# Attention's values in one stationary tile: two passes instead of three, and the sums of the probabilities added on GpSimd

## The chip, the cores and the metric

The kernel runs on one core of a Trainium2 chip. The time is the device time of one execution in microseconds, the median of several runs. The core's engines work side by side and are named as the profile names them: PE (TensorE, matrix products; PEld is its loading of the stationary operand), DVE (VectorE), ACT (ScalarE), POOL (GpSimd) and SP (SyncE, which issues most DMAs). Each engine works off its own queue in order and waits on semaphores for the others.

## The reference

A trunk of two layers on 1024 rows of 1024 numbers, in float32. Layer 0 mixes with a gated MLP, layer 1 with attention; each is followed by a channel mixer (an up-projection, a short convolution, a gate, a down-projection). The change lies in the attention:

```python
def one_chunk(args):
    c, qb = args
    start = c * CHUNK
    kb = lax.dynamic_slice_in_dim(kp, start, BAND, axis=1)
    vb = lax.dynamic_slice_in_dim(vp, start, BAND, axis=1)
    sc = jnp.einsum('bqhd,bkhd->bhqk', qb, kb).astype(jnp.float32) + bias
    ...
    p = jax.nn.softmax(sc, axis=-1).astype(vb.dtype)
    return jnp.einsum('bhqk,bkhd->bqhd', p, vb)
```

There are 16 heads of 64 numbers. Each chunk of 64 rows sees itself and the 8 chunks before it, so a block of 128 keys is seen by at most five blocks of 128 queries.

## The kernel before

**Precision.** PE multiplies in a format with fewer bits than float32 (`F32R`). So each operand is split into a high part (a cast, on ACT) and a low part (the difference, on DVE or POOL), and a product is made of three passes: high by high, low by high, high by low. The helper `split` does this (lines 137 to 140: `hi` by ACT, `lo` by DVE), which is why many rows of the profile bear L139 and L140.

**The attention's tiles.** Two heads make a pair `p` of 128 columns; `c` is 0 or 1 within the pair, and a head number is 2p + c. `rows[c]` gives the head's own 64 partitions and the other 64. The values of a pair come from a projection (`operand`, L1088 and around), are transposed on PE (`transpose_v`) and split into `vh` and `vl`. The stationary tile of a head and key block has 128 columns: 64 hold the head's values, the other 64 hold ones (in `VH`) or zeros (in `VL`). So the product of `VH` with the probabilities gives in 64 rows the weighted values and in the other 64 the sum of the probabilities, which the softmax divides by. The values of the second head are put into their tile by two DMAs (`stage_v`).

**A head's steps.** `Head.score(kb)` makes, for key block kb (0 to 7), the scores `st` of up to five query blocks (up to 640 columns) on PE, adds the bias near the diagonal on DVE, takes the exponential on ACT (tile `p`, two instructions), casts it to `ph` on ACT (L1269) and subtracts to `pl` on POOL (L1270). `Head.value(kb)` multiplies: for each half `t` of the 1024 query columns that the block touches, three passes into the PSUM tile `po` (L1286 `vh` by `ph`, L1288 `vl` by `ph`, L1290 `vh` by `pl`). The first half is complete with block 3, the second with block 7. Then `Pair.done` copies the sum of the probabilities to `den` (ACT, L1311) and the values to `o` (DVE, L1315); later, with delays counted in a modelled clock (`put_off`), `o` is multiplied by the reciprocal of `den`.

**The order of the work.** PE's order is written out by hand: `tick` counts a modelled time of PE, and what was put off is issued when its time has come. The other engines' queues are ordered by the framework's scheduler, which knows nothing of the chip's real times. The main loop goes over s, 16 heads by 8 blocks. A step issues the scores of block i, half of the step's projection matmuls (`fill`: those of the next pair's q, k and v), the row maxima of the next head (`mx`, DVE), then `value` of the block two steps back (`LAG = 2`), then the other half. A step has 12 projection matmuls in the first head of a pair and 6 in the second; about 5 in pair 0 and in the last pair, and 3 in the first half of head 13. The projections' weights come by DMA and are scaled by a gain on POOL (L159), one of 1024 columns per weight. The small PSUM tiles (`psS`: `st`, `mx`, transposes) rotate through four banks, `po` through two.

Of the kernel before, what the change touches and what calls it, by code (L numbers as in the profile page):

```python
# [10 lines left out]
F32 = mybir.dt.float32  # L11
F32R = mybir.dt.float32r
AF = mybir.ActivationFunctionType
ALU = mybir.AluOpType
# [4 lines left out]
P = 128  # L19
T = 1024  # L20
D = 1024
H = 512
KD = D // P
NB = T // P
# [5 lines left out]
LAG = 2  # L30
# [11 lines left out]
def f32(ap):  # L42
    return ap.bitcast(F32)
# [3 lines left out]
def trunk(ctx: ExitStack, tc: tile.TileContext, x, a_win, a_wv, a_wst, a_bs, a_wout, w_kv, w_q, w_o,  # L47
          f_win, f_wdown, bias, cst, consts, fgain, out):
    nc = tc.nc
    V, S, G = nc.vector, nc.scalar, nc.gpsimd  # L50
# [78 lines left out]
    ones_r = cp.tile([P, P], F32R, name="ones_r")  # L129
# [7 lines left out]
    def split(hi, lo, src, eng=V):  # L137

        behind[S] = S.copy(hi, src)  # L139
        return eng.tensor_tensor(lo, src, f32(hi), op=ALU.subtract)  # L140
# [444 lines left out]
    for t in range(2):  # L585
        for n in range(4):
            ps = psA("vps")
# [49 lines left out]
    for i, g in enumerate((0, 4, 1, 5, 2, 6, 3, 7)):  # L637
# [3 lines left out]
        for t in range(2):  # L641
            spatial(g, t)
            ps = psA("ups")
# [404 lines left out]
    rows = [(slice(0, 64), slice(64, P)), (slice(64, P), slice(0, 64))]  # L1048
# [19 lines left out]
    parts = {}  # L1068

    def operand(p, what, w, t):  # L1070

        hs = halves[t]
        if t == 0:
            if what == "v":
                parts[p, what] = [b1.tile([P, NB, 64], F32R, tag=f"v{n}", name=f"v{n}") for n in ("hi", "lo")]
            else:
                parts[p, what] = [bt.tile([P, T], F32R, tag=f"t{n}", name=f"t{n}") for n in ("hi", "lo")]
        hi, lo = parts[p, what]
        if p == 0:
            ps = ps2[what, t]  # L1080
        else:
            ps = psP("qkv")
            yield from products(ps, w, ys[t], range(KD), LAST)
        if what == "q":
            S.mul(hi[:, hs], ps, 0.125)
            V.scalar_tensor_tensor(lo[:, hs], ps, 0.125, f32(hi[:, hs]), op0=ALU.mult, op1=ALU.subtract)
        elif what == "k":
            S.copy(hi[:, hs], ps)  # L1088
            V.tensor_tensor(lo[:, hs], ps, f32(hi[:, hs]), op=ALU.subtract)
        else:  # L1090
            vT = b2.tile([P, H], F32, tag="vT", name="vT")
            S.copy(vT, ps)
            put_off(1.2, lambda: transpose_v(vT, t, hi, lo))

    def stage(hd, cs):

# [45 lines left out]
    LAST = KD - 1  # L1142
# [13 lines left out]
    with tc.tile_pool(name="b1", bufs=1, reuse_waits="tile") as b1, \  # L1156
# [2 lines left out]

        for place, n in ((QE, "qe"), (QS, "qs"), (KM, "km"), (KS, "ks")):  # L1160
            place.append(b1.tile([P, T], F32R, name=f"{n}1"))
        VH, VL = ([b1.tile([P, NB, P], F32R, name=f"{n}{c}") for c in range(2)] for n in ("vh", "vl"))
        constant_rows(1, lambda: b2.tile([P, H], F32, tag="o", name="e"))
        for c in range(2):
            oth = rows[c][1]
            G.memset(f32(VH[c][:, :, oth]), 1.0)
            G.memset(f32(VL[c][:, :, oth]), 0.0)

        def heads():

# [5 lines left out]
                    yield from operand(p, what, w, t)  # L1176
                w = nw

        def transpose_v(vT, t, hi, lo):
            pt = psS("vtr")  # L1180
            for i in range(4):
                nc.tensor.transpose(pt[:, i * P:(i + 1) * P], vT[:, i * P:(i + 1) * P], ident)
            ns = slice(t * 4, t * 4 + 4)
            ptv = pt.rearrange("p (n c) -> p n c", c=P)
            for c, vh, vl in ((0, VH[0][:, ns, 0:64], VL[0][:, ns, 0:64]), (1, hi[:, ns, :], lo[:, ns, :])):
                src = ptv[:, :, rows[c][0]]
                S.copy(vh, src)
                V.tensor_tensor(vl, src, f32(vh), op=ALU.subtract)

        def stage_v(p):  # L1190
            for dst, src in zip((VH[1], VL[1]), parts[p, "v"]):
                nc.sync.dma_start(f32(dst[:, :, 64:P]), f32(src))

        class Max:

# [38 lines left out]
        class Head:  # L1234


            def __init__(self, hd, bt, done):
                self.hd, self.c, self.bt, self.done = hd, hd % 2, bt, done
                self.po = [None, None]
                self.p = {}  # L1240

            def score(self, kb):
# [19 lines left out]
                marks[0] = V.tensor_tensor(pf[:, :n2], near[:, :n2], bt[:, :n2], op=ALU.add)  # L1262
                S.activation(pf[:, :n2], pf[:, :n2], AF.Exp)
# [5 lines left out]
                marks[1] = S.copy(ph[:, :n], pf[:, :n])  # L1269
                marks[2] = G.tensor_tensor(pl[:, :n], pf[:, :n], f32(ph[:, :n]), op=ALU.subtract)  # L1270
                self.p[kb] = (ph, pl)

            def value(self, kb):

                c, (ph, pl) = self.c, self.p.pop(kb)
                q0 = kb * P
                lo_end = q0 + min(5, NB - kb) * P
                for t, (a, b) in enumerate(((q0, min(lo_end, H)), (max(q0, H), lo_end))):
# [7 lines left out]
                    nc.tensor.matmul(d, VH[c][:, kb, :], ph[:, r], start=kb == 0, stop=False, skip_group_check=True)  # L1286
                    tick(d.shape[1])
                    nc.tensor.matmul(d, VL[c][:, kb, :], ph[:, r], start=False, stop=False, skip_group_check=True)  # L1288
                    tick(d.shape[1])
                    nc.tensor.matmul(d, VH[c][:, kb, :], pl[:, r], start=False, stop=last, skip_group_check=True)  # L1290
                    tick(d.shape[1])
                    if last:
                        self.done(c, t, self.po[t])

        class Pair:

# [2 lines left out]
                self.p = p  # L1299
                self.o, self.den = [None, None], [None, None]  # L1300

            def done(self, c, t, po):
# [4 lines left out]
                p = self.p  # L1307
                if p < LAST:

                    row = slice(oth.start, oth.start + 1)  # L1310
                    S.copy(self.den[t][row], po[row])  # L1311
                    nc.sync.dma_start(dens[p][t][0][c:c + 1], self.den[t][row])
                else:
                    S.copy(self.den[t][own], po[oth])
# [80 lines left out]
        mid, end = {2: (1,), 3: (3,), 4: (5,), 5: (7,)}, {1: (0,), 2: (2,), 3: (4,), 4: (6,)}  # L1395
        for s in range(NH * NB):
            hd, i = divmod(s, NB)
            p, c = divmod(hd, 2)
# [5 lines left out]
            n = (6 if c else 12) + (1 - 2 * c if i == 0 else 0)  # L1404
            if p == LAST - 1 and c:
                n = 3 if i < 4 else 6
            if p == 0:
                n = (144 - early) * (s + 1) // 16 - (144 - early) * s // 16
            if p == LAST:
                n = 5  # L1410
# [27 lines left out]
            if i == (LAG if p < LAST else 5) and c == 0:  # L1438
                stage_v(p)
            for _ in range(n // 2):  # L1440
                next(fill, None)
            if hd + 1 < NH:
# [189 lines left out]
```

## Time and profile before

| | us |
|---|---|
| median of 3 runs (2134.68 to 2136.11) | 2135.33 |
| span of the profiled execution | 2131.1 |
| median over that span | 4.2 |
| POOL L1270 `pl`, 128 instructions, busy | 161.1 |
| first and last pass L1290 start at | 987.0, 1409.8 |

The span runs from the first to the last instruction of the one execution that the profiler recorded; a run's time has some microseconds around it, and the profiled execution's own time is known only as this span. In the rows of the profile, a timeline's row gives the start, the duration, the engine, the line, the operation, what it writes and reads with the shapes, and, in brackets, how long the engine stood idle before it and who ended that. A row that begins with two times gives, for that stretch, each engine's busy time with its number of instructions, then the granted clock of PE as a share of full speed, the DMA share and GB/s.

### The profile page before, as it was taken

How to read it: one execution, taken by the hardware profiler on the slowest of the kernel's cores; microseconds unless marked ns; L12 is line 12 of the kernel's file. 1: busy time of each engine (PE TensorE's matmuls, PEld its weight loads, DVE VectorE, ACT ScalarE, POOL GpSimd, SP SyncE). 2: the span in 40 equal slices, each digit the busy share in tenths (PEclk: the TensorE clock that was granted, in tenths of full speed). 3: DMA queues.
4: the chain of work that ended last, by engine and by line, in shares of the span. 5: the costliest groups of instructions: out<-in, count | busy, mean ns of one | idle time of the engine just before them, and what ended most of it. 6: DMA issues, size and time to landing. Idle time of an engine off the chain costs nothing.

```text
span 2131.1 us, 28842 instructions
## 1 busy us (share of the span) xinstructions
PE 2116.7 (99%) x9944; PEld 1773.0 (83%) x9944; DVE 1545.7 (73%) x2311; ACT 1065.4 (50%) x1878; POOL 752.9 (35%) x530
## 2 busy tenths in 40 slices
PE   9999999999999999999999999999999999999998
PEld 8888877888888888888888888888888888888887
DVE  4188789888888856675665655665988888885576
ACT  6333555545455544555555555643545544454443
POOL 1075745242333412054545444421322323341020
PEclk9999999999999999999999999999999999999999
DMA  7257722354445976735554555663243545478653
GB/s 253 79 203 256 243 99 99 130 193 138 163 165 194 296 269 215 239 105 139 139 127 129 129 130 133 178 218 114 73 154 134 186 137 175 164 278 300 213 190 126
DMA packets 181450, 367.86 MB, mean 173 GB/s; under 512 B 42908, under 2 KB 43292, under 8 KB 181304
## 3 DMA queue, kind: packets, MB, share of 16 engines
q1 hardware_dynamic: 177128, 358.47, 51.8%
q10 hardware_dynamic: 4176, 7.55, 1.0%
q8 instruction: 78, 1.28, 0.3%
q14 instruction: 68, 0.56, 0.1%
HBM read 233.12 MB, written 103.40 MB: 158 GB/s over the span
## 4 chain that ended last, share of the span: by engine, by line
PE 93%; DVE 4%; POOL 1%; ACT 1%; issue 1%; DMA 0%; DVEq 0%; SPq 0%; POOLq 0%; ACTq 0%
PE up L995 10%; PE gate L995 10%; PE up L375 7%; PE up L377 7%; PE up L380 7%; PE gate L375 5%; PE gate L377 5%; PE gate L380 5%; PE vps L510 4%; PE qkv L184 4%; PE qkv L181 4%; PE qkv L188 4%; PE ups L181 1%; PE po L1290 1%; PE st L1256 1%; PE ups L184 1%
## 5 line engine op out<-in xcount | busy, mean ns | idle before, releaser
L140 DVE TENSOR_TENSOR wlo<-raw,whi 128x512 fp32r<-128x512 f32 (+1 forms) x395 | 343.7, 876 | 179.8 <-ACT whi L139 179.6
L139 ACT CAST whi<-raw 128x512 fp32r<-128x512 f32 (+1 forms) x395 | 245.0, 623 | 282.7 <-PE gate L995 198.5
L375 PE MATMUL up<-yh,whi 128*128 128x512 f32 x688 | 267.8, 389 | 0.0
L377 PE MATMUL up<-yh,wlo 128*128 128x512 f32 x688 | 267.8, 389 | 0.0
L1270 POOL TENSOR_TENSOR pl<-p,ph 128x640 fp32r<-128x640 f32 (+4 forms) x128 | 161.1, 1261 | 180.1 <-ACT ph L1269 134.4
L847 POOL TENSOR_TENSOR h<-a 128x512 f32<-128x512 f32 x44 | 80.6, 1832 | 398.7 <-DVE a L839 387.3
L375 PE MATMUL gate<-th,whi 128*128 128x512 f32 x496 | 193.9, 391 | 2.7 <-DVE gate L903 2.7
L377 PE MATMUL gate<-th,wlo 128*128 128x512 f32 x496 | 193.9, 391 | 0.0
L380 PE MATMUL up<-yl,whi 128*128 128x512 f32 x688 | 184.2, 389 | 0.0
L380 PEld LDWEIGHTS up<-yl,whi 128*128 128x128 f32 x688 | 129.2, 188 | 27.2 <-POOL yl L140 0.5
L375 PEld LDWEIGHTS up<-yh,whi 128*128 128x128 f32 x688 | 129.2, 188 | 27.1 <-ACT gate L886 0.3
L377 PEld LDWEIGHTS up<-yh,wlo 128*128 128x128 f32 x688 | 129.2, 188 | 26.8
L140 DVE TENSOR_TENSOR yl<-raw,yh 128x512 fp32r<-128x512 f32 x172 | 143.1, 834 | 8.4 <-ACT yh L139 8.2
L184 PE MATMUL qkv<-yh,wlo 128*128 128x512 f32 x336 | 134.3, 400 | 0.0
L380 PE MATMUL gate<-tl,whi 128*128 128x512 f32 x496 | 132.7, 389 | 0.0
L181 PE MATMUL qkv<-yh,whi 128*128 128x512 f32 x336 | 132.5, 394 | 0.0
L139 ACT CAST whi<-S 128x512 fp32r<-128x512 f32 x160 | 99.0, 619 | 65.0 <-PE up L380 59.0
L140 DVE TENSOR_TENSOR wlo<-S,whi 128x512 fp32r<-128x512 f32 x160 | 130.2, 814 | 0.0
L995 PE MATMUL up<-yl,whi 128*128 128x512 f32 (+1 forms) x312 | 120.6, 387 | 0.0
L995 PE MATMUL up<-yh,whi 128*128 128x512 f32 (+1 forms) x312 | 120.4, 386 | 0.0
L995 PE MATMUL gate<-yh,wlo 128*128 128x512 f32 (+1 forms) x312 | 120.4, 386 | 0.0
L995 PE MATMUL up<-yh,wlo 128*128 128x512 f32 (+1 forms) x312 | 120.3, 386 | 0.0
(306 smaller groups left out, 5274.6 us busy)
## 6 DMA issues: line engine op xcount, KB each, us to landing
raw<-in_f_win SPq DMA_DIRECT2D x88, 512.0 KB
gT<-h SPq DMA_DIRECT2D x88, 256.0 KB
h<-in_f_wdown SPq DMA_DIRECT2D x44, 512.0 KB
dS<-h SPq DMA_DIRECT2D x88, 256.0 KB
raw<-dS SPq DMA_DIRECT2D x40, 512.0 KB
raw<-gT SPq DMA_DIRECT2D x40, 512.0 KB
gB<-a SPq DMA_DIRECT2D x66, 256.0 KB
raw<-in_f_wdown SPq DMA_DIRECT2D x30, 512.0 KB
```

Of the source, the lines that this page charges most:

```text
L139: behind[S] = S.copy(hi, src)
L140: return eng.tensor_tensor(lo, src, f32(hi), op=ALU.subtract)
L181: nc.tensor.matmul(ps, wh[:, k, :], xs[k][0], start=k == 0, stop=False)
L184: nc.tensor.matmul(ps, wl[:, k, :], xs[k][0], start=False, stop=False)
L188: nc.tensor.matmul(ps, wh[:, k, :], xs[k][1], start=False, stop=k == last)
L375: nc.tensor.matmul(ps, wh[:, k, :], xs[k][0], start=first and k == 0, stop=False, skip_group_check=True)
L377: nc.tensor.matmul(ps, wl[:, k, :], xs[k][0], start=False, stop=False, skip_group_check=True)
L380: nc.tensor.matmul(ps, wh[:, k, :], xs[k][1], start=False, stop=k == 3, skip_group_check=True)
L510: nc.tensor.matmul(ps, a, b, start=k == i == 0, stop=k == KD - 1 and i == 2)
L847: G.tensor_tensor(B[n], x, B.get(y) if isinstance(y, str) else y, op=ALU.subtract)
L995: nc.tensor.matmul(ps[:, cs], w[:, ms], x[:, cs], start=q == i == 0 and p in (1, 6, 5, 4), stop=q == NP - 1 and i == 2, skip_group_check=True)
L1270: marks[2] = G.tensor_tensor(pl[:, :n], pf[:, :n], f32(ph[:, :n]), op=ALU.subtract)
```

## The change

The stationary tile of a head and key block now holds the high part of the values in the head's own 64 columns and the low part in the other 64. One pass with `ph` and one with `pl` then give high and low products in the two halves of `po`, and `Pair.done` adds the halves (ACT copies one half to `o`, DVE adds the other). The passes with `vl` are gone. The second head's tile is doubled (`V1`) instead of being filled by DMA, so `stage_v` is gone.

The sums of the probabilities are no longer a by-product. `score` adds each block's `p` on POOL into `sum[t]` (a copy for block 0, a memset for the second half, adds for the rest). After block 3 (first half) and block 7 (second half) the sum is split into `sumh` (ACT) and `suml` (DVE), and `total`, called at the end of `value` for block 3 and block 7, multiplies both with a tile of ones: two passes of 512 columns into a small PSUM bank, `den`.

```diff
-        VH, VL = ([b1.tile([P, NB, P], F32R, name=f"{n}{c}") for c in range(2)] for n in ("vh", "vl"))
+        V0, *V1 = (b1.tile([P, NB, P], F32R, name=f"v{n}") for n in ("0", "1a", "1b"))
...
-            for c, vh, vl in ((0, VH[0][:, ns, 0:64], VL[0][:, ns, 0:64]), (1, hi[:, ns, :], lo[:, ns, :])):
-                src = ptv[:, :, rows[c][0]]
+            for v, (own, oth) in zip(both, rows):
+                src, vh = ptv[:, :, own], v[:, ns, own]
                 S.copy(vh, src)
-                V.tensor_tensor(vl, src, f32(vh), op=ALU.subtract)
+                V.tensor_tensor(v[:, ns, oth], src, f32(vh), op=ALU.subtract)
...
                 self.p[kb] = (ph, pl)
+                for t, (a, b) in enumerate(self.ranges(kb)):
+                    if a >= b:
+                        continue
+                    d, e = self.sum[t][:, a - t * H:b - t * H], pf[:, a - q0:b - q0]
+                    if kb == t == 0:
+                        G.tensor_copy(d, e)
+                        G.memset(self.sum[1], 0.0)
+                    else:
+                        G.tensor_tensor(d, d, e, op=ALU.add)
+                    if kb == (NB - 1 if t else 3):
+                        self.parts = [b2.tile([P, H], F32R, tag=n, name=n, bufs=1) for n in ("sumh", "suml")]
+                        split(*self.parts, self.sum[t])
...
+            def total(self, t):
+                ps = psS("den")
+                for i in range(2):
+                    nc.tensor.matmul(ps, ones_r, self.parts[i], start=i == 0, stop=i == 1)
+                    tick()
+                return ps
...
-                    nc.tensor.matmul(d, VH[c][:, kb, :], ph[:, r], start=kb == 0, stop=False, skip_group_check=True)
+                    nc.tensor.matmul(d, self.v[:, kb, :], ph[:, r], start=kb == 0, stop=False, skip_group_check=True)
                     tick(d.shape[1])
-                    nc.tensor.matmul(d, VL[c][:, kb, :], ph[:, r], start=False, stop=False, skip_group_check=True)
-                    tick(d.shape[1])
-                    nc.tensor.matmul(d, VH[c][:, kb, :], pl[:, r], start=False, stop=last, skip_group_check=True)
+                    nc.tensor.matmul(d, self.v[:, kb, :], pl[:, r], start=False, stop=last, skip_group_check=True)
                     tick(d.shape[1])
                     if last:
-                        self.done(c, t, self.po[t])
+                        self.done(c, t, self.po[t], self.total(t))
...
-                    S.copy(self.den[t][row], po[row])
+                    S.copy(self.den[t][row], total[row])
...
-                V.tensor_copy(self.o[t][own], po[own])
+                S.copy(self.o[t][own], po[oth])
+                V.tensor_tensor(self.o[t][own], po[own], self.o[t][own], op=ALU.add)
```

Where things stand now, at three places of head 3 (the second head of pair 1). A row gives the line, the operation, what is written and read, and the shape; the number behind a name tells buffers apart. Rows of before have the lines of before, rows of the change its own.

PE, the step that scores block 5 and multiplies block 3; before, with `po_9879` the first half and `po_9883` the second:

```order
L1217 MATMUL mx_10004<-km0_8304,qe0_8302 128x384
L1286 MATMUL po_9879<-ph_9907,vh1_8621 128x128
L1288 MATMUL po_9879<-ph_9907,vl1_8623 128x128
L1290 MATMUL po_9879<-pl_9908,vh1_8621 128x128
L1286 MATMUL po_9883<-ph_9907,vh1_8621 128x512
L1288 MATMUL po_9883<-ph_9907,vl1_8623 128x512
L1290 MATMUL po_9883<-pl_9908,vh1_8621 128x512
```

and with the change (`po_9930` and `po_9933` are the two halves):

```order
L1209 MATMUL mx_10057<-km0_8304,qe0_8302 128x384
L1303 MATMUL po_9930<-ph_9956,v1b_8622 128x128
L1305 MATMUL po_9930<-pl_9957,v1b_8622 128x128
L1287 MATMUL den_10063<-sumh_9961,ones_r_75 128x512
L1287 MATMUL den_10063<-suml_9962,ones_r_75 128x512
L1303 MATMUL po_9933<-ph_9956,v1b_8622 128x512
L1305 MATMUL po_9933<-pl_9957,v1b_8622 128x512
```

The `vl` passes are gone, and the two products with ones stand directly behind block 3's product into the first half, ahead of its product into the second.

ACT, the same step (`p_9986` and `ph_9993` are block 5's); before:

```order
L1269 CAST ph_9944<-p_9937 128x512
L1187 CAST vh0_8620<-vtr_9964 128x4x64
L1187 CAST vhi_9789<-vtr_9964 128x256
L1263 ACTIVATE p_9986<-p_9986 128x256
L1266 ACTIVATE p_9986<-st_9987,cc_68 128x128
L1311 COPY den_9694<-po_9879 1x512
L1269 CAST ph_9993<-p_9986 128x384
L1263 ACTIVATE p_10024<-p_10024 128x256
```

and with the change (block 5 is `p_10038`, `ph_10045`; `sumh_9961` is the first half's sum):

```order
L1263 CAST ph_9997<-p_9990 128x512
L1183 CAST v0_8620<-vtr_10018 128x4x64
L1183 CAST v1a_8621<-vtr_10018 128x4x64
L1330 COPY o_9731<-po_9930 64x512
L1257 ACTIVATE p_10038<-p_10038 128x256
L1260 ACTIVATE p_10038<-st_10039,cc_68 128x128
L1263 CAST ph_10045<-p_10038 128x384
L139 CAST sumh_9961<-sum_9833 128x512
L1326 COPY den_9732<-den_10063 1x512
L1257 ACTIVATE p_10079<-p_10079 128x256
```

The copy of `o` from block 3's product comes first, then block 5's exponentials and cast, and only then `sumh`.

POOL, from block 1 to block 5 of head 3; before:

```order
L1270 TENSOR_TENSOR pl_9837<-p_9826,ph_9836 128x640
L159 TENSOR_TENSOR raw_10461<-raw_10461,cc_68 128x1024
L1270 TENSOR_TENSOR pl_9869<-p_9858,ph_9868 128x640
L1100 MEMSET qe1_8616 1x512
L1270 TENSOR_TENSOR pl_9908<-p_9897,ph_9907 128x640
L1270 TENSOR_TENSOR pl_9945<-p_9937,ph_9944 128x512
L1270 TENSOR_TENSOR pl_9994<-p_9986,ph_9993 128x384
```

and with the change, from block 1's `pl` on (`sum_9833` is the first half's sum, `sum_9834` the second's; ahead of these rows stand block 0's add, copy and `pl` and block 1's two adds):

```order
L1264 TENSOR_TENSOR pl_9881<-p_9870,ph_9880 128x640
L159 TENSOR_TENSOR raw_10537<-raw_10537,cc_68 128x1024
L1274 TENSOR_TENSOR sum_9834<-sum_9834,p_9907 128x384
L1264 TENSOR_TENSOR pl_9918<-p_9907,ph_9917 128x640
L1274 TENSOR_TENSOR sum_9833<-sum_9833,p_9907 128x256
L1100 MEMSET qe1_8616 1x512
L1264 TENSOR_TENSOR pl_9957<-p_9946,ph_9956 128x640
L1274 TENSOR_TENSOR sum_9834<-sum_9834,p_9946 128x512
L1264 TENSOR_TENSOR pl_9998<-p_9990,ph_9997 128x512
L1274 TENSOR_TENSOR sum_9833<-sum_9833,p_9946 128x128
L1274 TENSOR_TENSOR sum_9834<-sum_9834,p_9990 128x512
L1264 TENSOR_TENSOR pl_10046<-p_10038,ph_10045 128x384
```

The add that completes the first half's sum (`sum_9833`, 128 columns) stands behind block 4's `pl`.

More of the change, by code (lines that the diff above doesn't have):

```diff
@@ L1074, in operand @@
             if what == "v":
-                parts[p, what] = [b1.tile([P, NB, 64], F32R, tag=f"v{n}", name=f"v{n}") for n in ("hi", "lo")]
+                parts[p, what] = V0, V1[p % 2]
             else:
@@ L1092, in operand @@
             S.copy(vT, ps)
-            put_off(1.2, lambda: transpose_v(vT, t, hi, lo))
+            put_off(1.2, lambda: transpose_v(vT, t, (hi, lo)))
     def stage(hd, cs):
@@ L1161, in trunk @@
             place.append(b1.tile([P, T], F32R, name=f"{n}1"))
-        VH, VL = ([b1.tile([P, NB, P], F32R, name=f"{n}{c}") for c in range(2)] for n in ("vh", "vl"))
+        V0, *V1 = (b1.tile([P, NB, P], F32R, name=f"v{n}") for n in ("0", "1a", "1b"))
         constant_rows(1, lambda: b2.tile([P, H], F32, tag="o", name="e"))
[L1164 to L1167, printed above, removed]
         def heads():
@@ L1177, in heads, with transpose_v @@
                 w = nw
-        def transpose_v(vT, t, hi, lo):
+        def transpose_v(vT, t, both):
             pt = psS("vtr")
@@ L1184, in transpose_v @@
             ptv = pt.rearrange("p (n c) -> p n c", c=P)
-            for c, vh, vl in ((0, VH[0][:, ns, 0:64], VL[0][:, ns, 0:64]), (1, hi[:, ns, :], lo[:, ns, :])):
-                src = ptv[:, :, rows[c][0]]
+            for v, (own, oth) in zip(both, rows):
+                src, vh = ptv[:, :, own], v[:, ns, own]
                 S.copy(vh, src)
-                V.tensor_tensor(vl, src, f32(vh), op=ALU.subtract)
-        def stage_v(p):
-            for dst, src in zip((VH[1], VL[1]), parts[p, "v"]):
-                nc.sync.dma_start(f32(dst[:, :, 64:P]), f32(src))
+                V.tensor_tensor(v[:, ns, oth], src, f32(vh), op=ALU.subtract)
         class Max:
@@ L1240, in __init__ @@
                 self.p = {}
+                self.v = parts[hd // 2, "v"][self.c]
+                self.sum = [b2.tile([P, H], F32, tag=f"sum{t}", name="sum", bufs=1) for t in range(2)]
             def score(self, kb):
@@ L1271, in score, with ranges @@
                 self.p[kb] = (ph, pl)
+                for t, (a, b) in enumerate(self.ranges(kb)):
[10 more added lines that the diff above has]
+                        split(*self.parts, self.sum[t])
+            def ranges(self, kb):
+                q0 = kb * P
+                end = q0 + min(5, NB - kb) * P
+                return (q0, min(end, H)), (max(q0, H), end)
+            def total(self, t):
[4 more added lines that the diff above has]
+                return ps
             def value(self, kb):
@@ L1276, in value @@
                 q0 = kb * P
-                lo_end = q0 + min(5, NB - kb) * P
-                for t, (a, b) in enumerate(((q0, min(lo_end, H)), (max(q0, H), lo_end))):
+                for t, (a, b) in enumerate(self.ranges(kb)):
                     if a >= b:
@@ L1300, in __init__, with done @@
                 self.o, self.den = [None, None], [None, None]
-            def done(self, c, t, po):
+            def done(self, c, t, po, total):
                 own, oth = rows[c]
@@ L1310, in done @@
                     row = slice(oth.start, oth.start + 1)
-                    S.copy(self.den[t][row], po[row])
+                    S.copy(self.den[t][row], total[row])
                     nc.sync.dma_start(dens[p][t][0][c:c + 1], self.den[t][row])
                 else:
-                    S.copy(self.den[t][own], po[oth])
-                V.tensor_copy(self.o[t][own], po[own])
+                    S.copy(self.den[t][own], total[own])
+                S.copy(self.o[t][own], po[oth])
+                V.tensor_tensor(self.o[t][own], po[own], self.o[t][own], op=ALU.add)
                 if c == 0:
@@ L1437, in trunk @@
                 stage(hd + 2, halves[0])
-            if i == (LAG if p < LAST else 5) and c == 0:
-                stage_v(p)
             for _ in range(n // 2):
```

## Prediction

> **What bounds the kernel now.** I read the page's busy shares first, then the busy time of every engine in the stretch of the attention, then the list of who waited for whom on PE, and last the order of time of one head.
>
> ```profile
> PE 2116.7 (99%) x9944; PEld 1773.0 (83%) x9944; DVE 1545.7 (73%) x2311; ACT 1065.4 (50%) x1878; POOL 752.9 (35%) x530
> 985.00:1411.00 426.00, 424.51 (x2271) 368.60 (x2270) 256.17 (x656) 248.67 (x528) 204.51 (x172) 1.00 0.53 137
> PE gate L375 <- DVE gate L903: 2.7, 1, 2.7
> PE gate L249 <- DVE acc L238: 1.0, 1, 1.0
> ```
>
> The second row is the stretch from the first product with the values to the last (PE, PEld, DVE, ACT, POOL, then the granted clock). PE is busy 424.5 of 426 us there; the other four have idle time, POOL more than half. The last two rows head the list of PE's waits in the whole program: the longest is 2.7 us, the next 1.0, and both lie outside this stretch (L375 is the channel mixer's, L249 the norm's). So every matmul that goes here shortens the span, and every new wait of PE lengthens it: nothing hides either.
>
> **What goes and what comes on PE.** A matmul's duration in the trace overlaps its neighbours; what one is worth is the distance between starts. In head 3 (the second head of pair 1):
>
> ```profile
> 1065.22 0.39 PE L1290 MATMUL po<-pl,vh 128*128 128x512 f32 x1
> 1065.45 0.22 PE L1286 MATMUL po<-ph,vh 128*128 128x128 f32 x1
> 1065.51 0.28 PE L1288 MATMUL po<-ph,vl 128*128 128x128 f32 x1
> 1065.62 0.27 PE L1290 MATMUL po<-pl,vh 128*128 128x128 f32 x1
> ...
> 1068.40 0.34 PE L1288 MATMUL po<-ph,vl 128*128 128x384 f32 x1
> 1068.58 0.34 PE L1290 MATMUL po<-pl,vh 128*128 128x384 f32 x1
> 1068.76 0.28 PE L1286 MATMUL po<-ph,vh 128*128 128x256 f32 x1
> 1068.88 0.29 PE L1288 MATMUL po<-ph,vl 128*128 128x256 f32 x1
> 1069.00 0.28 PE L1290 MATMUL po<-pl,vh 128*128 128x256 f32 x1
> ```
>
> One pass is worth 0.23 us at 512 columns, 0.18 at 384, 0.12 at 256, 0.11 at 128. A head has three passes with `vl` of each width (the blocks' ranges are cut at column 512), so 3 x 0.64 = 1.92 us go, in 16 heads 30.7 us. The products with ones are four of 512 columns a head, 4 x 0.23 = 0.92 us, in 16 heads 14.7 us. Net: **-16 us**.
>
> **What the sums cost on POOL.** POOL gets, per head, one copy and one memset of 512 columns and adds of 2x512, 3x384, 3x256 and 3x128. No add of this kind is in the trace; the nearest rows are `pl`, also two f32 inputs from SBUF, and the one in-place sum of the program:
>
> ```profile
> 1061.54 1.57 POOL L1270 TENSOR_TENSOR pl<-p,ph 128x640 fp32r<-128x640 f32 x1 [4.20 <-ACT ph L1269]
> 1072.96 1.30 POOL L1270 TENSOR_TENSOR pl<-p,ph 128x512 fp32r<-128x512 f32 x1 [1.71 <-issue]
> 1076.82 1.01 POOL L1270 TENSOR_TENSOR pl<-p,ph 128x384 fp32r<-128x384 f32 x1 [2.56 <-ACT ph L1269]
> 1078.87 0.74 POOL L1270 TENSOR_TENSOR pl<-p,ph 128x256 fp32r<-128x256 f32 x1 [1.04 <-issue]
> 1056.89 0.46 POOL L1270 TENSOR_TENSOR pl<-p,ph 128x128 fp32r<-128x128 f32 x1 [0.53 <-ACT ph L1269]
> 1065.84 1.90 POOL L159 TENSOR_TENSOR raw<-raw,cc 128x1024 f32<-128x1024 f32 x1 [0.15 <-DMA raw<-in_w_q]
> 1069.21 0.52 POOL L1100 MEMSET qe<- 1x512 f32 x1
> L238 POOL TENSOR_TENSOR acc<-acc,sq x8: 1292/1303/1833, 228.1 to 2056.3; 128x512 f32<-128x512 f32 x8
> ```
>
> The in-place sum has the same 1.30 us as `pl` of that width, so I take `pl`'s. The copy lies between the memset (0.52) and a sum (1.30); I take 0.9, the middle, being like neither. A head's additions are then 0.9 + 0.5 + 2.6 + 3.0 + 2.2 + 1.4 = 10.6 us, and POOL goes from 204.5 to about 374 us of the stretch: it still fits on average. It doesn't fit in the first half of a head. Second heads have half the projection work between their steps, and from `p` of block 0 to that of block 4 pass some 11.4 us (the rows 1061.54 and 1072.96). I add up POOL's rows in the changed order, head 3, from the moment at which `p` of block 0 is there:
>
> ```profile
> 1060.29 0.41 ACT L1263 ACTIVATE p<-p 128x256 f32<-128x256 f32 x1
> 1075.14 0.42 ACT L1263 ACTIVATE p<-p 128x256 f32<-128x256 f32 x1 [1.18 <-DVE p L1262]
> ...
> 1075.71 0.56 ACT L1311 COPY den<-po 1x512 f32<-1x512 f32 x1
> 1076.18 0.51 ACT L1269 CAST ph<-p 128x384 fp32r<-128x384 f32 x1
> 1075.18 0.22 PE L1286 MATMUL po<-ph,vh 128*128 128x128 f32 x1
> 1075.24 0.28 PE L1288 MATMUL po<-ph,vl 128*128 128x128 f32 x1
> ```
>
> Start 1060.7. Block 0: add 0.46, copy 0.9, `pl` 1.57 (1063.6). Block 1: 0.74 + 1.02 + 1.57 (1067.0). The weight's gain 1.90 and block 2: 1.02 + 1.57 (1071.5), 0.74. Memset 0.52, block 3: `pl` 1.57 (1074.3), add of 512 1.30, then `pl` of block 4 1.30, and only then the add of 128 columns that completes the first half's sum, 0.46: **1077.4**. The `pl` of blocks 0 to 3 are each in time or within 0.3 us of it.
>
> **The new wait.** PE reads the first half's sum right behind block 3's product into the first half. That product starts at 1075.24 now and some 0.7 us earlier then (the five blocks ahead of it, from head 2's block 6 on, lose 1.18 us of `vl` passes, and head 2's ones add 0.46); the second product with ones could start at 1074.9. It needs `sumh` (ACT) and `suml` (DVE), and both stand late in their queues. On ACT, `sumh` stands behind the copy of `o` from that same product, behind block 5's two exponentials and its `ph`: product done 1074.8, copy 0.5 (as the `den` copy, 1075.71 to 1076.18), exponentials and `ph` 1.1 (1075.14 to 1076.69 less that copy), so ACT is free at 1076.5; POOL's 1077.4 comes later. For `sumh`, a cast of 128x512, and `suml` on DVE these rows are the nearest:
>
> ```profile
> 1153.60 0.61 ACT L139 CAST oh<-o 128x512 fp32r<-128x512 f32 x1
> 1153.83 1.57 POOL L1270 TENSOR_TENSOR pl<-p,ph 128x640 fp32r<-128x640 f32 x1 [1.13 <-ACT ph L1269]
> 1154.24 1.71 DVE L140 TENSOR_TENSOR ol<-o,oh 128x512 fp32r<-128x512 f32 x1
> 1155.88 0.68 DVE L140 TENSOR_TENSOR wlo<-raw,whi 128x512 fp32r<-128x512 f32 x1
> ```
>
> The cast takes 0.61, so `sumh` ends at 1078.0. A subtraction like `suml` took 0.68 us with POOL at rest and 1.71 beside a running POOL operation, ending 0.55 after it (1155.40, 1155.95). In the changed order POOL is by then in an add of 512 columns (1077.4 to 1078.7), so `suml` ends at 1079.2 and **PE has waited 4.3 us**. With the copy at 0.52 and no such meeting it is 3.2, with 1.30 4.7; I take 4.0. Behind `sumh` ACT has queued the copy of `den` and block 6's exponential, behind `suml` DVE has block 6's bias sum: all need work that PE does after its wait, so they add nothing.
>
> Heads 1, 3, 5, 7, 9, 11 and 13 have `sumh` at about this place (in 1, 11 and 13 the copy of `o` stands elsewhere, POOL's sum doesn't): 7 x 4.0 = 28. First heads have 12 projection matmuls a step and `sumh` ahead of block 5: no wait, but for head 0, whose steps are as short.
>
> ```profile
> 984.15 0.42 ACT L1263 ACTIVATE p<-p 128x256 f32<-128x256 f32 x1 [1.05 <-DVE p L1262]
> 990.85 0.44 PE L1290 MATMUL po<-pl,vh 128*128 128x384 f32 x1 [0.35 <-POOL pl L1270]
> 996.97 0.28 PE L1288 MATMUL po<-ph,vl 128*128 128x128 f32 x1
> ```
>
> There PE waits for `pl` already, and from 984.6 the same sum puts block 1's `pl` (with a gain of 1.90 ahead of it) at 992.8 and the half sum at 1000.0, `suml` at 1001.8: 2.6 us of wait at block 1 and 2.8 at the sum, 5.4. Heads 14 and 15 have no gain and `sumh` ahead of block 5; an estimate from head 3's sum less these is 1.3 each. Together 28 + 5.4 + 2.6 = **36 us**.
>
> **The clock.** The one long wait of the kernel before tells what a wait brings besides itself:
>
> ```profile
> 355.25 0.62 PE L375 MATMUL gate<-th,whi 128*128 128x512 f32 x1 [2.72 <-DVE gate L903]
> ...
> 358.65 1.20 PE L380 MATMUL gate<-tl,whi 128*128 128x512 f32 x4
> 356.00:358.00 2.00, 2.00 (x6) 1.51 (x5) 2.00 (x4) 1.07 (x1) 0.00 (x0) 0.50 0.81 241
> ```
>
> After 2.72 us without work the granted clock was 0.50 and eight matmuls, 355.25 to 358.65, stood 0.43 apart where 0.23 is usual: 1.6 us more. The eight long waits are longer than that one, though the first product with ones cuts each in two; I take six of eight with this price, 10 us, bounds 0 and 9 x 1.6 = 14. The Trainium skill (TensorE: Matmul & The Clock Gate, What's actually happening) lets the clock fall after a whole idle window of some 3.4 us and asks for no longer gaps; by that rule 2.72 us would not have done it, and the trace shows that it did. By the rule the sum would leave these 10 us out.
>
> **Edits that I cost at nothing.** ACT gets two `sumh` and two copies of `o` a head, about 2.3 us of the 26.6 that a head lasts; ACT is idle 42% of the stretch. DVE gets two `suml`, the copy of `o` becomes a sum of the same width. The cover is PE's own work between a step's scores and its use two steps on; were it gone, ACT's part would be 16 x 2.3 = 37 us at most. The sum of ones holds one of four small PSUM banks until ACT has copied `den`; `po`'s bank is read once more, with some 15 matmuls (3 us) until the next head needs it. The 16 DMAs of the values leave SP's queue: no wait of PE names them. The transposes stay.
>
> **Sum.** -16 + 36 + 10 = +30; the span 2131.1 becomes 2161. The runs' median 2135.33 lies 4.2 above the span of the profiled one, so about **2165 us**, 1.4% slower. This case alone spans 2150 to 2182 (waits of 3.2 to 4.7, clock 0 to 14).
>
> **Rivals.**
> 1. The clock never falls, because the product between the two halves of each wait keeps the activity up. For it: a product stands between two waits of some 2.5 and 1.5 us, each shorter than the 2.72, and the longest wait next to that one was 1.0. Against: their sum is longer. -16 + 36 = +20: 2155. The Trainium skill's rule of a whole idle window leads to this case too.
> 2. POOL is not late (its adds fill the gaps of 1 to 4 us that stand before `pl` now), and only ACT's queue counts: 2.9 us in heads 3, 5, 7 and 9, 2.4 in 13, 1.9 in 1 and 11, 18 in all: -16 + 18 = +2, 2137. Against it stands the sum of the rows above.
> 3. Faster: `sumh` and `suml` are done when PE comes to them. Place: the product with ones behind block 3 in second heads. It decides when the waits together stay under 16 us, some 1.8 in each of nine heads; all hidden gives 2135.3 - 16 = 2119. For it: POOL is 52% idle. Against: PE's order is fixed, and ACT's queue alone holds 2 to 2.9 us between that product and `sumh`.
> 4. POOL never catches up: 27 us a pair now, 21 more, and each of some 14 DVE subtractions and products from SBUF a pair blocks it 0.55 (8 us), in all the 56 that a pair lasts; with 0.1 us between its 60 instructions, 62, and seven pairs at +7 against 55 give 2185.
>
> **Chances.** Forecast 0.62, rival 1 0.18, rival 2 0.08, rival 3 0.06, rival 4 0.06. 0.2% (4.3 us) is about what a measurement of this kernel can tell from no change: faster 0.06, same 0.08, slower 0.86. The range 2143 to 2183 takes in the forecast and rival 1 with their bounds and leaves out the other three.
>
> **What would show it.** In the changed profile: PE waiting for `suml` and `sumh` some 36 us in all, about 4 in each second head; POOL at about 370 us between the first and last product with the values; granted clock under 1.00 in the slices of the attention; the `v` passes at the distances above. I am wrong if PE's waits for the sums are under 16 us, if POOL's adds take much less than `pl` of their width, or if the lost time lies outside the attention.

## The result, and the profile after

The changed kernel takes 2199.85 us (median of 4 runs, 2197.05 to 2202.2), the kernel before 2135.72 beside it (4 runs): a ratio of 1.030, 95% interval 1.0286 to 1.0311. The forecast was 2165 with a range of 2143 to 2183: the sign is right, the size is not (+64 instead of +30).

The profiled run of after spans 2200.4 us. First its busy shares, then the stretch of the attention, from 985 us to behind the last product with the values (PE, PEld, DVE, ACT, POOL, granted clock), then rows of the list of PE's waits in that stretch (sum in us, times, longest):

```profile
PE 2131.3 (97%) x9816; PEld 1772.5 (81%) x9816; DVE 1599.9 (73%) x2343; ACT 1101.8 (50%) x1942; POOL 922.2 (42%) x734
985.00:1479.50 494.50, 440.66 (x2164) 369.89 (x2163) 316.30 (x692) 287.49 (x596) 373.65 (x379) 0.94 0.41 111
PE den L1287 <- DVE suml L140: 22.9, 9, 4.2
PE den L1287 <- ACT sumh L139: 17.5, 8, 2.6
PE mx L1209 <- DVE mb L1205: 4.3, 5, 1.5
PE po L1305 <- POOL pl L1264: 4.0, 4, 1.5
...
PE vtr L1178 <- DVE mb L1205: 1.9, 1, 1.9
```

Before, PE was idle for 1.5 of 426 us there; now for 53.8 of 494.5. Of these, 40.4 stand ahead of the products with ones, and some 13 at places where nothing was forecast. The clock fell to 0.94 on average. POOL is where it was expected, at 374 us.

Now the place of the forecast's sum in a second head. The order of time of after in head 7, at the end of block 3, with PE, ACT, DVE and POOL apart (the POOL row of 1220.84 joins two additions, block 3's of 128 columns that completes the first half's sum, and block 4's of 512):

```profile
1221.99 0.49 PE L1287 MATMUL den<-sumh,ones_r 128*128 128x512 f32 x1 [2.53 <-ACT sumh L139]
1225.11 0.79 PE L1287 MATMUL den<-suml,ones_r 128*128 128x512 f32 x1 [2.62 <-DVE suml L140]
1225.70 0.63 PE L1303 MATMUL po<-ph,v1b 128*128 128x512 f32 x1
1226.12 0.63 PE L1305 MATMUL po<-pl,v1b 128*128 128x512 f32 x1
...
1219.50 0.58 ACT L1330 COPY o<-po 64x512 f32<-64x512 f32 x1 [1.42 <-PE po L1305]
1220.80 0.51 ACT L1263 CAST ph<-p 128x384 fp32r<-128x384 f32 x1
1221.32 0.62 ACT L139 CAST sumh<-sum 128x512 fp32r<-128x512 f32 x1
...
1220.95 3.50 DVE L1213 SCALAR_TENSOR_TENSOR mb<-ma,cc,mb 128x6 f32<-128x6 f32 x1
1224.37 0.68 DVE L140 TENSOR_TENSOR suml<-sum,sumh 128x512 fp32r<-128x512 f32 x1
...
1219.62 1.25 POOL L1264 TENSOR_TENSOR pl<-p,ph 128x512 fp32r<-128x512 f32 x1
1220.84 1.68 POOL L1274 TENSOR_TENSOR sum<-sum,p 128x128 f32<-128x128 f32 x2
1222.49 0.98 POOL L1264 TENSOR_TENSOR pl<-p,ph 128x384 fp32r<-128x384 f32 x1
1223.44 0.98 POOL L1274 TENSOR_TENSOR sum<-sum,p 128x384 f32<-128x384 f32 x1
1229.51 0.74 POOL L1274 TENSOR_TENSOR sum<-sum,p 128x256 f32<-128x256 f32 x1 [5.09 <-ACT p L1257]
```

`sumh` came at the place that was forecast, behind the copy of `o` and block 5's `ph`; POOL completed the sum at the same moment, about 1221.3 (an addition of 128 columns lasts 0.44 us at least). `suml` took only 0.68, but DVE couldn't begin it: an operation on six columns, `mb` (L1213, the row maxima of the next head), stood ahead and lasted 3.50 us. POOL ran one operation behind the other from 1219.62 (and before) to 1224.42, and `mb` ended when that run ended; three POOL operations had begun and ended since DVE stood at it. The same `mb` lasts 3.5 to 4.6 us close ahead of `suml` in six of the seven second heads 1 to 13 (not in 11). Two operations write `mb`: this one (L1213) and the row maximum itself (L1205), which reads the bank that `mx` wrote. Here is the row of all 16 of L1213, first in the kernel before and then in after (min/median/max in ns):

```profile
L1221 DVE SCALAR_TENSOR_TENSOR mb<-ma,cc,mb x16: 206/227/980, 978.1 to 1379.8; 128x6 f32<-128x6 f32 x16
```

```profile
L1213 DVE SCALAR_TENSOR_TENSOR mb<-ma,cc,mb x16: 344/984/4599, 982.8 to 1444.1; 128x6 f32<-128x6 f32 x16
```

It isn't held until POOL has a gap every time. In head 2, one `mb` ended with the addition that it met, though POOL's next operation began at once:

```profile
1069.54 0.99 DVE L1213 SCALAR_TENSOR_TENSOR mb<-ma,cc,mb 128x6 f32<-128x6 f32 x1
1069.03 1.48 POOL L1274 TENSOR_TENSOR sum<-sum,p 128x384 f32<-128x384 f32 x1
1070.45 1.02 POOL L1264 TENSOR_TENSOR pl<-p,ph 128x384 fp32r<-128x384 f32 x1
```

Of the 16, eight go this way and six are passed by three or four POOL operations; what decides between the two is not shown.

And the clock behind head 7's wait, in windows laid along it (the number ahead of the last two of a row is the granted clock):

```profile
1222.00:1224.20 2.20, 0.49 (x1) 0.18 (x1) 2.20 (x1) 0.00 (x0) 2.20 (x3) 0.99 0.00 0
1224.20:1227.60 3.40, 2.50 (x6) 2.01 (x7) 0.85 (x2) 0.57 (x1) 0.22 (x1) 0.50 0.00 1
1227.60:1231.00 3.40, 3.40 (x12) 2.52 (x10) 0.42 (x1) 0.82 (x2) 1.43 (x2) 0.50 0.06 6
1231.00:1232.00 1.00, 1.00 (x8) 0.86 (x7) 0.08 (x1) 0.26 (x1) 0.23 (x1) 1.00 0.00 0
```

The half clock lasts 6.8 us, not 3.4: the rows of PE from 1225.70 on stand 0.43 apart instead of 0.23, up to 1231. In the whole stretch there are nine such times, eight of them at the waits for the sums and one at 1432 us: three last 3.4 us, five 6.8 and one 10.2. Their sum, over windows laid along all nine (the granted clock is 0.50 in each):

```profile
sum 54.62, PE 41.74 PEld 32.35 DVE 18.94 ACT 11.28 POOL 19.65; mean PE 4.64 PEld 3.59 DVE 2.10 ACT 1.25 POOL 2.18
```

PE was busy 41.7 us at half clock, which at the full one would have been 21. The length of a wait doesn't tell alone whether the clock falls: in head 0, waits of 1.76 and 0.64 us were followed by 3.4 us at 0.50, in head 14 a wait of 2.69 us was followed by 1.00.

### The profile page after: what moved, and what is told of

The parts are those of the page before. It is cut to its first block, busy times and chain, and to the rows that moved or that the text cites. A ratio compares the mean times of both kernels' runs of the same rounds, so it can differ in the third digit from the quotient of the medians.

```text
span 2200.4 us, 28877 instructions
## 1 busy us (share of the span) xinstructions
PE 2131.3 (97%) x9816; PEld 1772.5 (81%) x9816; DVE 1599.9 (73%) x2343; ACT 1101.8 (50%) x1942; POOL 922.2 (42%) x734
## 4 chain that ended last, share of the span: by engine, by line
PE 85%; DVE 8%; POOL 2%; issue 2%; ACT 2%; DMA 1%; SPq 0%; DVEq 0%; POOLq 0%; ACTq 0%
PE up L995 9%; PE gate L995 9%; PE up L375 7%; PE up L377 7%; PE up L380 7%; PE gate L375 5%; PE gate L377 5%; PE gate L380 5%; PE vps L510 4%; PE qkv L184 3%; PE qkv L188 3%; PE qkv L181 3%; PE ups L181 1%; PE ups L184 1%; PE ups L188 1%
## 5 line engine op out<-in xcount | busy, mean ns | idle before, releaser
L1274 POOL TENSOR_TENSOR sum<-sum,p 128x256 f32<-128x256 f32 (+3 forms) x176 | 157.9, 907 | 77.9 <-ACT p L1260 34.9
```

The lines of the kernel that those rows point to most:

```text
L1274: G.tensor_tensor(d, d, e, op=ALU.add)
```

## The experiments

The theory that they test: PE waits for `sumh` and `suml` because POOL is late with the first half's sum and because DVE often gets no turn beside a POOL that runs without a gap; each such wait brings 6.8 us at half clock. Each kernel is the changed one with the edit shown; times are compared with the kernel before, run beside it.

**Without the additions.** The additions and the copy of block 0 are gone, both sums are set to 1.0.

```diff
                     if kb == t == 0:
-                        G.tensor_copy(d, e)
-                        G.memset(self.sum[1], 0.0)
-                    else:
-                        G.tensor_tensor(d, d, e, op=ALU.add)
+                        for s in self.sum:
+                            G.memset(s, 1.0)
```

> Leaves out all additions of probabilities and the copy of block 0 on GpSimd; both sums are set to 1.0 instead, and splitting them, the products with ones and the division stay. Theory (GpSimd's lateness and DVE's wait for it cost about two thirds of the wait, ScalarE's order one third): the waits for suml all but vanish, those for sumh stay at 1 to 2.5 us in heads 3, 5, 7 and 9, 18 us or fewer in all, and the time is 2135 - 16 + 10 to 18, with up to 10 us of half clock: 2130 to 2147. Rival (ScalarE's order alone sets it): the wait stays at 40 us and the time at 2185 or more.

Measured: 2133.6 us, once, beside 2134.7. No wait for `sumh` or `suml` is left. The stretch, and the longest of PE's waits in it:

```profile
985.00:1411.50 426.50, 417.30 (x2160) 354.63 (x2159) 287.74 (x690) 285.88 (x593) 222.64 (x201) 1.00 0.47 128
PE st L1250 <- DMA qe<-mr: 3.7, 6, 0.8
```

So the 64 us come with the additions, as work for POOL and as something to wait for (both sums are there from block 0 on). The smaller part of the expectation fell: not even `sumh` was waited for. But that says nothing of ACT's order by itself, since a sum that is ready at block 0 lets the scheduler put `sumh` half a head earlier into ACT's queue. The second finding is that even with sums for nothing the change gains some 1 us at most, which one run can't tell from none, where 16 had been reckoned: PE is idle 9.2 us here, 7.7 more than before, in many small waits.

**The passes alone.** No sums, no split, no products with ones (the divisor is taken from `po`).

```diff
-                        self.done(c, t, self.po[t], self.total(t))
+                        self.done(c, t, self.po[t], self.po[t])
```

> Leaves out the sums, their split and the products with ones; what divides is taken from the values' own product, so only the change of three passes to two stands. Theory: the 192 passes are worth 30.7 us, so 2135 - 30.7 = 2104. Rival (a pass is worth less, because it covered work that PE then waits for): above 2112.

Measured: 2115.3 us beside 2136.9. The rival's condition (above 2112) is met: 21.6 us are gained instead of 30.7.

```profile
985.00:1392.00 407.00, 399.23 (x2094) 341.69 (x2093) 256.21 (x658) 268.71 (x562) 202.79 (x172) 1.00 0.50 134
PE st L1249 <- DMA qe<-mr: 2.2, 3, 0.9
PE mr L1218 <- DVE mb L1213: 1.8, 1, 1.8
PE po L1290 <- DVE o L1318: 1.5, 3, 0.7
```

The passes themselves went nearly as reckoned: the distances from one start to the next, added up over all passes into `po`, fall from 91.7 to 62.6 us, by 29.1. But PE is idle for 7.8 us of the stretch instead of 1.5. By the waits that are named here, the products with `vl` had covered the way from `mx` over `mb` and `mr` to the next head's `qe`, and the release of `po`.

**Work in the wait.** Products whose result is thrown away stand ahead of the products with ones, in second heads.

```diff
+FILL = (0, 20)
...
             def total(self, t):
                 ps = psS("den")
+                for _ in range(FILL[self.c]):
+                    nc.tensor.matmul(ps, ones_r, QE[self.c][:, 0:H], start=True, stop=True)
```

> Adds 20 products of 512 columns, some 4.6 us of work whose result is thrown away, ahead of each product with ones in second heads; nothing is left out. It separates the clock from the wait: 8 heads x 2 halves x 4.6 = 74 us of work are added, of which only the half that stands at the first half's sum (37 us) can lie in a wait. Theory (two windows of 3.4 us at half clock behind each wait cost some 25 us): no windows at half clock are left in second heads, waits there shrink by some 30 us, and the time is 2199.9 + 74 - 30 - 25 = about 2219. Rival (the half clock costs what I forecast, 10 us): about 2234; rival (the clock costs nothing, since PE would have waited in that time anyway): about 2244.

Measured: 2222.3 us, once, beside 2134.7.

```profile
985.00:1494.30 509.30, 488.57 (x2454) 410.70 (x2453) 311.20 (x689) 285.35 (x593) 374.29 (x379) 1.00 0.39 108
```

PE does some 73 us more (320 products, 0.23 apart) and idles 20.7 us instead of 53.8. 2199.9 + 73 - 33 would be 2240; the other 18 us are put down to the clock, which is back at 1.00 but for one time of 3.4 us. That fits the 21 us from the half-clock rows of after, and lies between the theory's 25 and the forecast's 10.

**The products with ones later.** `total` and the division are put off by 4.5 us of PE's modelled time for the first half and 2.0 for the second; the copy of `o` stays; the split of the second half moves to `value(6)`.

```diff
+DELAY = (4.5, 2.0)
...
-                        self.done(c, t, self.po[t], self.total(t))
+                        self.done(c, t, self.po[t], lambda t=t, parts=self.parts: self.total(t, parts))
...
+                S.copy(self.o[t][own], po[oth])
+                V.tensor_tensor(self.o[t][own], po[own], self.o[t][own], op=ALU.add)
+                put_off(DELAY[t], lambda: self.divide(c, t, total()))
...
-                waits = (8.0, 8.0) if stays else (9.0, 9.0 if p < LAST - 1 else 6.5)
+                waits = (6.0, 6.0) if stays else (9.0, 9.0) if p < LAST - 1 else (7.0, 5.5)
```

> Moves the two products with ones, and the division that needs them, 2.0 to 4.5 us of PE work behind the last block of each half; nothing is left out. Theory (PE's 40 us of waits for the sums, and the half clock behind them, are the loss): the waits for sumh and suml all but vanish, the granted clock stays near 1.00, and 2199.9 us falls by 40 + 25 or so, to between 2120 and 2140. Rival (GpSimd's load itself slows the blocks, through pl and the banks of mx): the products wait no more, but PE waits for pl and mx instead, and the time stays above 2165.

Measured: 2167.8 us, ratio 1.016 (1.0143 to 1.0177): 32 us less than after, but 28 more than the upper end of the theory; the rival's time (above 2165) is met.

```profile
PE st L1251 <- DVE mb L1206: 9.6, 6, 2.0
PE mr L1219 <- DVE mb L1214: 8.0, 6, 1.8
PE po L1311 <- POOL pl L1265: 5.8, 9, 1.4
PE den L1291 <- DVE suml L141: 1.8, 1, 1.8
```

The wait for the sums is all but gone (3.0 us), and others have come in its place. L1214 is the `mb` that is held on DVE as before (median 1050 ns); 8.0 us end with it, 9.6 with the row maximum (L1206) and 5.8 with `pl`.

**The low part on POOL.**

```diff
-                        split(*self.parts, self.sum[t])
+                        split(*self.parts, self.sum[t], G)
```

> suml is subtracted on GpSimd in place of VectorE, 32 operations of about 1.3 us more for GpSimd and 32 fewer for VectorE; results stay. Theory (VectorE's turn is what makes suml late): suml follows the operation that GpSimd is in, the second wait of a head shrinks from 2.6 to under 2 us, the waits for the sums from 40 to about 30 us, and the time is 2180 to 2200. Rival (GpSimd's lateness alone): 32 x 1.3 = 42 us more on GpSimd make the sums later, the waits rise above 45 us and the time above 2205.

Measured: 2200.1 us, once, the same as after.

```profile
PE den L1287 <- POOL suml L140: 21.0, 10, 3.0
PE den L1287 <- ACT sumh L139: 18.1, 9, 2.6
```

Both expectations missed. Taken off DVE, `suml` stands in POOL's own queue and is as late: 39.1 us of waits instead of 40.4. So taking `suml` away from DVE doesn't help by itself: POOL's queue makes it as late.

**The additions on DVE**, in the changed order and with the later products with ones.

```diff
-                        G.tensor_copy(d, e)
+                        V.tensor_copy(d, e)
...
-                        G.tensor_tensor(d, d, e, op=ALU.add)
+                        V.tensor_tensor(d, d, e, op=ALU.add)
```

> All additions of probabilities, and the copy of block 0, move from GpSimd to VectorE; order and results stay. Theory (VectorE gets no turn while GpSimd runs one operation behind the other, and that makes both suml and mb late): by the subtraction of 512 columns at rest, 0.68 us, the additions cost VectorE some 5 us a head, 82 in all, which fit (315 of 490 us busy before, part of that time being such waits); GpSimd falls back to about 220 us of the stretch, mb takes 0.2 to 0.5 us again, waits for sumh and suml fall to under 18 us, and the time is 2130 to 2150. Rival (whichever engine adds is late, by the load alone): VectorE has more to do than GpSimd had idle time for, scores wait for it, and the time stays above 2165.

> As the kernel with the later products with ones (2167.8), with the additions and the copy on VectorE. There, 23 us of PE's waits were for mb and pl in place of the sums. Theory (these were VectorE's lack of a turn beside GpSimd): the waits for mb and pl fall below 8 us and the time is 2115 to 2132, faster than the kernel before. Rival (VectorE's load alone makes mb late): waits for mb stay above 15 us and the time above 2145.

Measured: 2158.2 us, ratio 1.0098 (1.008 to 1.0116), and 2162.1, ratio 1.0121 (1.0105 to 1.0137). In the first of the two:

```profile
985.00:1437.40 452.40, 426.86 (x2144) 356.19 (x2144) 384.03 (x879) 283.89 (x592) 223.67 (x187) 0.98 0.44 120
PE mx L1202 <- DVE mb L1205: 7.6, 10, 2.2
PE mx L1209 <- DVE mb L1205: 4.3, 3, 1.6
PE po L1305 <- POOL pl L1264: 3.6, 1, 3.6
...
PE den L1287 <- DVE mb L1205: 0.9, 1, 0.9
```

```profile
L1213 DVE SCALAR_TENSOR_TENSOR mb<-ma,cc,mb x16: 203/224/995, 978.9 to 1398.5; 128x6 f32<-128x6 f32 x16
```

With POOL back at 224 us, `mb` takes 224 ns again and the waits for the sums are gone (40.4 to 0.9): the lack of a turn came from POOL's additions. 42 us of the 64 go with them; how much of it by the lack of a turn and how much by POOL's lateness this kernel doesn't tell, since it takes away both. The time lies between the two expectations. What remains, PE's 25.5 idle us, mostly ends with DVE: at 384 of 452 us busy, it is late with the row maxima, whose banks `mx` then waits for. The later order adds nothing to this: at 2162.1 its theory missed, and its rival is met (15 us of waits for the two `mb`).

**The additions divided**, those of the first half on DVE, the others on POOL; in the changed order and in the later one.

```diff
-                        G.tensor_tensor(d, d, e, op=ALU.add)
+                        (G if t else V).tensor_tensor(d, d, e, op=ALU.add)
```

> The additions into the first half's sum (384, 256 and 128 columns a head) go to VectorE, those into the second half's and the copy of block 0 stay on GpSimd; order and results stay. Theory (GpSimd is late with the first half's sum in second heads, and its running on without a gap holds VectorE): GpSimd has 16 x 2.4 = 39 us less, VectorE about 16 x 1.2 = 19 more; the first half's sum is there before block 3's product, waits for sumh and suml fall from 40 to under 10 us, the half clock behind them goes, mb is still held at times, and the time is 2140 to 2160. Rival (the load on the two engines together is what counts, wherever it lies): mb and pl are as late as with all additions on one engine, and the time is above 2158.

> The same division of the additions between VectorE and GpSimd, with the later products with ones (which alone gave 2167.8, with all additions on VectorE 2162.1). Theory: neither engine is late, waits in the stretch fall to about those of the kernel without additions (8.5 us), and the time is 2134 to 2150, not faster than the kernel before, since without any additions it is 2133.6. Rival: the waits for mb stay above 15 us, as in the two kernels named, and the time above 2155.

Measured: 2160.1 us, ratio 1.0102 (1.0082 to 1.0122), and 2157.8, ratio 1.010 (1.0085 to 1.0115). The waits for the sums are 5.5 us in the first of them, as the theory has it, but its time lies at the theory's upper end, where the rival begins. The second has the rival's time, though its waits for `mb` come to 12.5 us and not to 15. The longest of PE's waits in it:

```profile
PE st L1251 <- DVE mb L1206: 8.8, 8, 3.7
PE po L1311 <- POOL pl L1265: 4.6, 5, 2.2
PE mx L1203 <- DVE mb L1206: 2.3, 2, 1.8
```

In five placements and orders, then, the additions cost 24 to 34 us over the kernel without them, in their place in the change 66. No version with its sums beat the kernel before. By the kernel without additions (2133.6 beside 2134.7) a better place for them could at best draw level in this order of the products; no run leaves the additions out in the later order.

## Why the prediction was right in its sign and wrong in its size

Right: PE loses what the stretch of the attention loses; POOL's 374 us; the place and the cause of the wait for `sumh` (17.5 us in eight heads; in head 7 behind ACT's queue and POOL's last addition at the same moment, where the sum for head 3 had ACT free 0.9 us before POOL). Rival 2 (POOL not late) and rival 3 (hidden) fell with the list of waits, rival 1 (the clock never falls, since a product stands between the two waits) with the clock's rows, rival 4 since POOL still has gaps.

That the waits for both parts come to 40.4 us where 36 were forecast is in part luck. The seven second heads have 5.0 us each instead of 4.0, head 0 has 2.4 instead of 5.4. In head 7 the wait is 2.53 us for `sumh` and 2.62 for `suml`, where the sum for head 3 had 3.1 and 1.2.

Three terms of the sum were off, in the span of the stretch as follows.

1. **The clock, 10 us: the step that failed most for its size.** I took 1.6 us for each of six waits from the one wait of before, after which a single window of 3.4 us ran at half. Behind the new waits it is mostly two; the first still holds part of the wait. PE is busy 440.66 us in 2164 instructions, and 417.30 in 2160 in the kernel without additions, whose clock stays at 1.00 there: 22 us beyond the four instructions. The half-clock rows give 21, the kernel with work in the wait 18. My upper bound of 14 was too low.
2. **The waits, 36 us with all else at nothing: the step that failed most in microseconds.** PE idles 52 us more than before. The sums are 40.4 of it, by a mechanism that I had only in part: I let a subtraction on DVE end 0.55 us after the POOL operation it meets, where in fact the small `mb` ahead of it is passed by three or four POOL operations. The other 13 us, which I put at nothing, stand where I named "PE's own work between a step's scores and its use two steps on" as the cover: 7.1 end with `mb`, 4.0 with POOL's `pl`, 1.7 with `o`. In the kernels without additions and with the passes alone, the idle time that comes with the removal of the passes is 6 to 8 us. But it stands at other places, above all ahead of `st`, which waits for `qe`; so how much of the 13 has this cause, and how much the load of POOL, stays open.
3. **The passes and the products with ones, -16 us.** By the distances between starts in the kernel without additions, the passes give some 30 and the products with ones cost some 17 (64 of them, 0.26 apart on average, not 0.23): -13.

Together -13 + 52 + 22 = 61 of the 69 us between the two spans. Of the rest some 4 lie ahead of the stretch, where after has one more half-clock window, near 300 us, and 2 us more idle time; the kernel without additions, though as fast as before, has that window too, so it is no effect of the additions. The last 4 us are not placed. The medians are only 64 apart: the two profiled executions lie some 5 us further from each other. The profiled run of after took 1.8 us more than its span, so the 4.2 us by which the forecast went from the span to the median held some 2 us of the scatter of single runs.

Some numbers of the prediction don't follow from its own terms. With waits of 4.7 us in seven heads, the 8 us of the others and 14 for the clock, the case's upper end is 2174, not 2182; the shorter wait of 3.2 us comes to 3.4; and the lower end of the range, 2143, is worked out nowhere, since the forecast's case begins at 2150 and rival 1 stands at 2155. The range was wider than its terms give, and the time still lay outside it.

Not separated: how much of the wait for `sumh` is ACT's order and how much POOL's lateness, because ACT's queue changes by itself when the sums are ready earlier.

## What to carry to other kernels

On an engine that is busy all the time, count what a removed instruction had covered, not only its own time: here 6 to 8 of some 30 us came back as small waits. Before work goes to an engine that "has room", look for the small operations on its neighbours that stop while it runs, and ask how long it runs without a gap at worst, not how long one operation lasts. And price long waits of PE with the clock that they cost behind them: here about half as much again, at waits of some 5 us in two parts.

## What the runs showed of the hardware

A DVE operation with two inputs from SBUF doesn't always take turns with POOL. `mb`, 0.22 us by itself, lasted up to 4.6 us, over several POOL operations, and in head 7 ended with the last of them before a gap; in head 2 (0.99 us) it did take its turn between two. The Trainium skill (SBUF — State Buffer, SBUF: two separate sides) says that whichever of the two starts first holds the shared ports for the whole instruction while the other blocks. The trace agrees that DVE blocks, but three POOL operations came in ahead of the waiting `mb` (3.50 us), where by first come, first served it would have waited for the end of the one that it met, some 0.4 us.

The granted clock fell at 2.53 and 2.62 us without work that were parted by one product (head 7), at 1.76 and 0.64 us parted so (head 0), and after 2.72 us in the kernel before; it stayed at 1.00 behind 2.69 us (head 14). In after it stayed at half for one to three stretches of 3.4 us.
